# Expert rows fetched and results combined by indirect DMAs in place of one-hot products

## The chip, the cores and the metric

The kernel runs on one core of a Trainium2 chip, as one program. The metric is device microseconds. Engines are named as in the profile: PE is TensorE, PEld its weight loads, DVE is VectorE, ACT is ScalarE, POOL is GpSimd, and SP is SyncE, whose queue starts nearly all transfers.

## The reference

Two layers over 256 tokens of 1024 channels, all float32. Each layer mixes tokens and then channels; the first layer's channel part is dense, the second's is a mixture of eight experts of which each token takes two. Cut to what matters here:

```python
def swiglu(h, wg, wu, wd):
    return (jax.nn.silu(h @ wg) * (h @ wu)) @ wd

def moe(h, router, wg, wu, wd):
    logits = (h @ router).astype(jnp.float32)
    vals, idx = lax.top_k(logits, TOP_K)
    w = jax.nn.softmax(vals, axis=-1)
    gates = jnp.sum(jax.nn.one_hot(idx, N_EXPERTS, dtype=jnp.float32) * w[..., None], axis=-2)
    y = jnp.zeros_like(h)
    for e in range(N_EXPERTS):
        y = y + gates[..., e:e + 1].astype(h.dtype) * swiglu(h, wg[e], wu[e], wd[e])
    return y
...
        h = rmsnorm(x, ln2_g[l]) * (1.0 + sc2) + sh2
...
            f = moe(h, moe_router[j], moe_w_gate[j], moe_w_up[j], moe_w_down[j])
        x = x + g2 * f
    return rmsnorm(x, final_g)
```

An expert's three matrices are 1024 x 3072 each, 37.7 MB; all eight are 302 MB of the 424.68 MB that the page counts.

## The kernel before

**Weights.** All matrices stream from DRAM in chunks of 1 MB (128 x 2048 f32), in a fixed order, on SyncE's queue; `fetch` starts the next chunk, and the transfer waits there until the readers of its buffer are done. There are ten buffers named `raw`, one `raw2`, and one made of two halves (`raw3`, and the tile `xn1`): twelve in the experts. Where a product has three passes, each half chunk (512 KB, a *part*) is cut into a rounded `wh` by ScalarE (line 147) and a remainder `wl = raw - wh` by VectorE (line 148), the second part of the split. `split_next` issues the first; the second goes on the list `rests` and is issued by `split_rest`. `refill` keeps four parts cut ahead of TensorE, and issues the remainders of the earlier call, not its own; `piece` issues one if TensorE's program is about to need it. `mm3` (lines 208 to 210) makes wh, wl and the low part of the input into three passes.

**Order of the work.** No scheduler sets it. A tick (`tick`) is counted before each group of products; `after(n, fn)` puts work n ticks later, and `spread(ticks, steps)` runs the steps of a generator at such distances. What is issued at a tick stands in each engine's program there, and each engine runs its own program in order.

**Experts.** `route` computes the router, the two best experts of a token and their gates, and `sort` ranks the experts by their number of tokens, so that the slots j = 0 to 7 (E0 to E7 in this text) take them by size: slots 0, 2 and 3 are big (128 rows, three passes through wh and wl), 5 and 6 are middle ones (96 rows) and 1, 4 and 7 are half ones (64 rows). Middle and half experts multiply the f32 chunks as they lie (lines 889, 911, 942, 954, 974 and 981) and have no split. A big one has 72 ticks of six products, a half one 72 ticks, a middle one 84.

**Gather.** `gather` makes for one or two experts a one-hot of their rows (`pl`), multiplies the normed tokens, cut into `xh` and `xl`, by it (line 1484: 32 products of up to 256 columns), scales and shifts the result on ScalarE into the expert's inputs, and transposes the one-hots (lines 1500 and 1505) for the way back. It is called for E0 ahead of the loop, and in E0, E2, E4 and E6 for the two experts behind each (in E6 for E7 alone).

**Scatter.** When an expert's down products are done, `scatter` (line 1576, a big one), `scatter_half` (line 1525) or `scatter_mid` (line 1551) multiplies its result `y` by the transposed one-hot, and VectorE adds the product, times the token's gate, to the residual `x`. This is spread over the ticks of the next expert. E7's scatter, the norm and the output stand at the end. An overflow path, for more tokens than slots, stands behind and is not run with these inputs.

Of the kernel before, what the change touches and what calls it, by code (L numbers as in the profile page):

```python
# [49 lines left out]
QUAD = P // 4  # L50

# [17 lines left out]
C_ID, C_TRI, C_IOTA, C_SEL, C_TIE, C_PLACE = 0, 128, 256, 384, 388, 396  # L69
C_N = 404  # L70
# [4 lines left out]
class Kernel:  # L75
# [34 lines left out]
    def fetch(self):  # L110
# [3 lines left out]
        more = i % (RAW_BUFS + 2) - RAW_BUFS if i >= 0 else -1  # L114
# [3 lines left out]
        else:  # L118
            e[1] = [self.moe.tile([P, PIECE], F32, tag="raw3", name="raw", bufs=1),
                    self.core.tile([P, PIECE], F32, tag="xn1", name="raw")]  # L120
# [92 lines left out]
    def setup(self):  # L213
# [41 lines left out]
        self.places = cst[:, C_PLACE:C_PLACE + NE]  # L255
        self.par = par
# [1043 lines left out]
    def route(self, out):  # L1300
        nc, small = self.nc, self.small
        xh = [self.core.tile([P, D], F32R, tag=f"hh{t}", name="xh") for t in range(NT)]
        xl = [self.core.tile([P, D], F32R, tag=f"hl{t}", name="xl") for t in range(NT)]
# [21 lines left out]
        nc.scalar.activation(xh[0], out[0], AF.Copy)  # L1325
        gate2(4 - TICKS[1]["fill"][2])
        out.append(self.normed(1, y))
        modulated(0, ())
# [11 lines left out]
        nc.scalar.activation(xh[1], out[1], AF.Copy)  # L1340
# [3 lines left out]
        nc.vector.tensor_tensor(xl[0], out[0], xh[0].bitcast(F32), op=ALU.subtract)  # L1344
# [22 lines left out]
        nc.vector.tensor_tensor(xl[1], out[1], xh[1].bitcast(F32), op=ALU.subtract)  # L1367
# [13 lines left out]
        self.spread([9, 3], self.sort(mem))  # L1381
        return rank, gate, xh, xl
# [42 lines left out]

    def place(self, rank, e, base, out, dt_cols):
# [12 lines left out]
    def slots(self, single):  # L1439

        pl = self.work.tile([P, NT, 2 * P], F32R, tag="pl", name="pl", bufs=1)
        if single:
            self.nc.gpsimd.memset(pl[:, :, P:].bitcast(F32), 0.0)
        return pl

# [479 lines left out]
```

## Time and profile before

| | us |
|---|---|
| median of three runs | 1279.29 |
| lowest and highest | 1275.89, 1280.31 |
| the profiled execution | 1276.7 |
| its span | 1274.8 |
| TensorE busy | 1223.6 (96%) |
| VectorE busy | 687.7 (54%) |
| ScalarE busy | 554.2 (43%) |
| GpSimd busy | 21.3 (2%) |

The span is the profiled execution on the core; 1.9 us lie around it. Transfers moved 424.68 MB, 333 GB/s on average. Shares are averages over stages with different limits, so they are read by stretch.

The stages by time: layer 0's mix to 170 us, its dense part to 360, layer 1's mix to 486, the router to 507, then E0 to 617, E1 to 691, E2 to 797, E3 to 903, E4 to 977, E5 to 1081, E6 to 1185, and E7 with the end to 1274.8.

### The profile page before, as it was taken

Reading aid. Unit: us, or ns where it says so; the run is one execution under the profiler, and the core shown is the slowest. Engines: PE = TensorE matmul, PEld = TensorE weight load, DVE = VectorE, ACT = ScalarE, POOL = GpSimd, SP = SyncE. Lnnn points to the kernel's source line nnn. Section 1 sums busy time; section 2 is a strip of 40 time slices with the busy share of each in tenths; the row PEclk is TensorE's granted clock in tenths of the full one; section 3 lists DMA queues with packets and bytes.
Section 4 is the critical chain, followed back from the end, with each engine's and each line's share of the span. In section 5 each row is a group of like instructions: output and inputs, shape, how many; then the busy total and the mean of one; then the engine's idle time right before and its main releaser. Section 6 shows DMA issues by size and latency. Waiting matters only on the chain.

```text
span 1274.8 us, 19410 instructions
## 1 busy us (share of the span) xinstructions
PE 1223.6 (96%) x7702; PEld 813.0 (64%) x7702; DVE 687.7 (54%) x992; ACT 554.2 (43%) x809; POOL 21.3 (2%) x40
## 2 busy tenths in 40 slices
PE   5899999999999989999998999999999999999995
PEld 4777799999978768788434888888433333333332
DVE  4677687776567766988404889999401001100102
ACT  3466454444444945888203888788210000010001
POOL 1000100000000000000000000000000000000001
PEclk9999999999999988999999999999999999999998
DMA  9976788887544346899999999999999999998994
GB/s 374 418 304 229 275 315 300 308 298 293 191 183 168 131 171 256 300 338 343 364 418 419 419 418 419 391 363 366 343 419 418 418 419 417 364 375 348 418 418 194
DMA packets 63427, 424.68 MB, mean 333 GB/s; under 512 B 7734, under 2 KB 7990, under 8 KB 15072
## 3 DMA queue, kind: packets, MB, share of 16 engines
q1 hardware_dynamic: 63072, 423.28, 84.5%
q8 instruction: 62, 1.02, 0.3%
q14 instruction: 37, 0.30, 0.1%
q0 software_dynamic: 256, 0.09, 0.0%
HBM read 422.29 MB, written 1.05 MB: 332 GB/s over the span
## 4 chain that ended last, share of the span: by engine, by line
PE 81%; DMA 7%; DVE 6%; ACT 4%; issue 1%; SPq 0%; POOL 0%; POOLq 0%; DVEq 0%; ACTq 0%
PE gps L889 4%; PE ups L889 4%; PE gps L580 4%; PE gps L582 4%; PE gps L578 4%; PE gps L942 3%; PE yps L981 3%; PE ups L942 3%; PE bps L954 3%; DMA raw<-i_md 3%; DMA raw<-i_mu 3%; PE ups L209 2%; PE yps L209 2%; PE ups L208 2%; PE yps L210 2%; PE ups L210 2%
## 5 line engine op out<-in xcount | busy, mean ns | idle before, releaser
L148 DVE TENSOR_TENSOR wl<-raw,wh 128x1024 fp32r<-128x1024 f32 x344 | 408.2, 1220 | 57.6 <-ACT wh L147 55.3
L147 ACT ACTIVATE wh<-raw 128x1024 fp32r<-128x1024 f32 x344 | 359.7, 1060 | 168.0 <-PE gps L580 55.9
L580 PE MATMUL gps<-hl,wh 128*128 128x256 f32 x384 | 96.5, 284 | 0.7 <-DVE hl L566 0.7
L578 PE MATMUL gps<-hh,wh 128*128 128x256 f32 x384 | 96.7, 284 | 0.1
L580 PEld LDWEIGHTS gps<-hl,wh 128*128 128x128 f32 x384 | 72.8, 190 | 1.3 <-DVE hl L566 1.1
L578 PEld LDWEIGHTS gps<-hh,wh 128*128 128x128 f32 x384 | 72.8, 190 | 0.5 <-DVE hh L565 0.3
L900 DVE TENSOR_TENSOR sgs<-sgs,ups 128x512 f32<-128x512 f32 x9 | 6.2, 688 | 120.6 <-PE ups L889 120.6
L911 PE MATMUL yps<-raw,hTs 128*64 128x512 f32 x288 | 66.9, 596 | 2.3 <-DMA raw<-i_md 2.1
L947 DVE TENSOR_TENSOR sgm<-sgm,ups 128x512 f32<-128x512 f32 x6 | 4.1, 688 | 116.6 <-PE ups L942 116.6
L889 PE MATMUL ups<-raw,ef 128*64 128x512 f32 x288 | 65.3, 594 | 0.8 <-DMA raw<-i_mu 0.8
L889 PE MATMUL gps<-raw,ef 128*64 128x512 f32 x288 | 66.0, 598 | 0.0
L582 PE MATMUL gps<-hh,wl 128*128 128x256 f32 x384 | 61.7, 283 | 0.0
L209 PE MATMUL gps<-wl,eh 128*128 128x512 f32 x144 | 57.0, 396 | 1.5 <-DVE wl L148 1.5
L208 PE MATMUL gps<-wh,eh 128*128 128x512 f32 x144 | 57.0, 396 | 1.2 <-ACT wh L147 1.2
L208 PE MATMUL yps<-wh,fh 128*128 128x512 f32 x144 | 58.0, 402 | 0.0
L209 PE MATMUL ups<-wl,eh 128*128 128x512 f32 x144 | 56.9, 395 | 0.5 <-DVE wl L148 0.5
L209 PE MATMUL yps<-wl,fh 128*128 128x512 f32 x144 | 56.7, 394 | 0.4 <-DVE wl L148 0.3
L208 PE MATMUL ups<-wh,eh 128*128 128x512 f32 x144 | 56.9, 395 | 0.0
L210 PE MATMUL gps<-wh,el 128*128 128x512 f32 x144 | 56.4, 391 | 0.0
L210 PE MATMUL yps<-wh,fl 128*128 128x512 f32 x144 | 56.3, 391 | 0.0
L210 PE MATMUL ups<-wh,el 128*128 128x512 f32 x144 | 56.3, 391 | 0.0
L582 PEld LDWEIGHTS gps<-hh,wl 128*128 128x128 f32 x384 | 52.8, 190 | 0.0
(329 smaller groups left out, 2038.8 us busy)
## 6 DMA issues: line engine op xcount, KB each, us to landing
raw<-i_mu SPq DMA_DIRECT2D x92, 1024.0 KB, 10.5
raw<-i_md SPq DMA_DIRECT2D x88, 1024.0 KB, 11.8
raw<-i_mg SPq DMA_DIRECT2D x84, 1024.0 KB, 9.5
raw<-i_ada SPq DMA_DIRECT2D x48, 1024.0 KB, 7.5
raw<-i_win SPq DMA_DIRECT2D x20, 1024.0 KB, 9.2
raw<-i_fg SPq DMA_DIRECT2D x12, 1024.0 KB, 6.8
raw<-i_fu SPq DMA_DIRECT2D x12, 1024.0 KB, 6.9
raw<-i_fd SPq DMA_DIRECT2D x12, 1024.0 KB, 6.5
```

The lines of the kernel that those rows point to most:

```text
L147: nc.scalar.activation(wh, raw, AF.Copy)
L148: self.rests.append(lambda: nc.vector.tensor_tensor(wl, raw, wh.bitcast(F32), op=ALU.subtract))
L208: mm(out, lhsT=xh, rhs=wh, start=start, stop=False)
L209: mm(out, lhsT=xh, rhs=wl, start=False, stop=False)
L210: mm(out, lhsT=xl, rhs=wh, start=False, stop=stop)
L578: self.nc.tensor.matmul(out, lhsT=w, rhs=hh[:, k, :], stop=False, start=k == 0 and (len(ks) == NK or m + j == 0))
L580: self.nc.tensor.matmul(out, lhsT=w, rhs=hl[:, k, :], start=False, stop=False)
L582: self.nc.tensor.matmul(out, lhsT=wl[:, j * len(ks) + i, :], rhs=hh[:, k, :], start=False, stop=k == NK - 1 and (len(ks) == NK or m + j == 1))
L889: nc.tensor.matmul(ps[c * HALF:(c + 1) * HALF, :], lhsT=eh[:, k, :], rhs=w[c][i // 2][:, i % 2, :], start=k == 0, stop=k == NK - 1)
L911: self.nc.tensor.matmul(y[n * HALF:(n + 1) * HALF, :], lhsT=hT[:, b, c * HALF:(c + 1) * HALF], rhs=w[n][b // 2][:, b % 2, :], start=i == 0 ...
L942: nc.tensor.matmul(ps[q(2 * c + s), :], lhsT=eh[:, k, q(s)], rhs=ws[w][c][i // 2][:, i % 2, :], start=k == 0, stop=k == NK - 1)
L954: nc.tensor.matmul(bp[q(2 * w + c), :], lhsT=eh[:, k, q(2)], rhs=ws[w][c][i // 2][:, i % 2, :], start=k == 0, stop=k == NK - 1)
```

## The change

*Way in.* The normed tokens are written to DRAM (`rows_in`) as soon as they are there. `sort` makes, after the ranks, a list of token numbers for each slot (14 products of one column, `tokps`) and casts it to integers. The first expert is still gathered by one-hot products, in f32 and without the cut. For the others, GpSimd issues an indirect DMA that brings the slot's rows (64, 96 or 128 of 4 KB) from `rows_in` into `gx`; eight transposes on TensorE (line 1534) turn them, 12 ticks behind the issue for the first of a pair.

*Way out.* An expert's result is multiplied by the output gate and written to its place in `rows_out` in DRAM by GpSimd's DMAs. `sort` also computes for each token the two rows at which its results lie (`where`) and their gates (`mine`). In E7, six ticks in, four indirect DMAs of 128 rows bring these back; 28 ticks later VectorE adds them to `x` in four operations. E7's own result is still scattered by products.

*Weights.* A thirteenth buffer is made of the tiles `hl0` and `hl1`, which `xl` held. The remainder `wl` is issued by VectorE directly after its `wh`, not a `refill` later.

```diff
-GATHER = [18, 7, 10]
-SCATTER = [1, 1, 1, 3, 2, 2, 1, 1, 3, 2, 2]
-SCATTER_S = [1, 1, 1, 2, 2, 2, 2]
-SCATTER_M = [1, 2, 1, 2, 2, 2, 2]
+LISTS = [9, 3, 3, 2, 3]
+GATHER = [22, 12, 2, 3, 2, 3, 2]
+STORE = [1, 1, 2, 2]
+COMBINE = [6, 28, 1]
...
+SLOTS = [P if b else HALF + QUAD * m for b, m in zip(BIG, MID)]
+BASE = [sum(SLOTS[:j]) for j in range(NE)]
...
-        more = i % (RAW_BUFS + 2) - RAW_BUFS if i >= 0 else -1
+        more = i % (RAW_BUFS + 3) - RAW_BUFS if i >= 0 else -1
...
+            if more == 1:
+                e[1] = [self.core.tile([P, PIECE], F32, tag=f"hl{h}", name="raw") for h in range(2)]
...
     def piece(self, n):
-        if len(self.rests) >= len(self.ready):
-            self.split_rest()
         return [w.rearrange("p (a b) -> p a b", a=n) for w in self.ready.pop(0)]
     def refill(self, most=1 + AHEAD):
-
-        old = len(self.rests)
         while len(self.ready) < most and self.spos < self.limit and self.split_at(self.spos * PIECE // RAW):
-            self.split_next(False)
-        for _ in range(old):
-            self.split_rest()
+            self.split_next()
...
+        self.keep(0, out[0])
...
+        self.spread(LISTS, self.sort(mem))
...
+    def keep(self, t, xn):
...
+        self.nc.gpsimd.dma_start(self.rows_in[t * P:(t + 1) * P], xn)
...
+        one = [self.core.tile([P, NE, P], F32, tag=f"hh{t}", name="one") for t in range(NT)]
+        rankm = self.small.tile([P, NT, NE], F32, tag="rankm", name="rankm", bufs=1)
+        nc.vector.tensor_scalar(rankm, self.rankp, -1.0, None, op0=ALU.add)
+        for t in range(NT):
+            nc.vector.tensor_tensor(one[t], self.iota[:, None, :].to_broadcast([P, NE, P]),
+                                    rankm[:, t, :, None].to_broadcast([P, NE, P]), op=ALU.is_equal)
+        yield
+        ps = self.psum.tile([P, NE], F32, tag="tr", name="tokps")
+        for j in range(1, NE):
+            for t in range(NT):
+                nc.tensor.matmul(ps[:, j:j + 1], lhsT=one[t][:, j, :], rhs=self.tok[:, t:t + 1], start=t == 0, stop=t == 1)
+        self.tokens = const.tile([P, NE], U32, tag="tokens", name="tokens")
+        nc.vector.tensor_copy(self.tokens[:, 1:], ps[:, 1:])
...
+        for i in range(2):
+            eq = self.small.tile([P, NT, NE], F32, tag="eq", name="eq", bufs=1)
+            nc.vector.tensor_tensor(eq, key, top[:, :, i:i + 1].to_broadcast([P, NT, NE]), op=ALU.is_equal)
+            nc.vector.tensor_tensor(eq, eq, ok, op=ALU.mult)
+            nc.vector.tensor_reduce(self.mine[:, i, :], eq, axis=AX.X, op=ALU.add)
+            nc.vector.tensor_scalar(top[:, :, i:i + 1], top[:, :, i:i + 1], -1.0, 0.0, op0=ALU.add, op1=ALU.max)
+            nc.vector.tensor_copy(self.where[:, i, :], top[:, :, i])
...
-                for n, (src, t) in enumerate(((xh, 0), (xl, 0), (xh, 1), (xl, 1))):
-                    nc.tensor.matmul(ps[:, i, :], lhsT=src[t][:, bs], rhs=pl[:, t, :], start=(n == 0),
-                                     stop=(n == 3))
...
+                for t in range(NT):
+                    nc.tensor.matmul(ps[:, i, :], lhsT=xn[t][:, bs], rhs=pl[:, t, :], start=t == 0, stop=t == 1)
...
+    def gather(self, js):
+        nc, work = self.nc, self.work
+        got = []
         for n, j in enumerate(js):
-            if MID[j]:
-
-                tp = self.psum.tile([P, 2 * NT, P], F32, tag="tr", name="plT")
-                for t in range(NT):
-                    for i, w in enumerate((HALF, QUAD)):
-                        src = pl[:, t, n * P + i * HALF:n * P + i * HALF + w].bitcast(F32)
-                        for r in range(0, P, w):
-                            nc.tensor.matmul(tp[r:r + w, i * NT + t, :], lhsT=src, rhs=self.ident, start=True, stop=True)
-                pt = work.tile([P, 2 * NT, P], F32, tag="el", name="pt4", bufs=2)
-            else:
+            w = SLOTS[j]
+            gx = self.core.tile([P, D], F32, tag=f"hh{n}", name="gx")
+            nc.gpsimd.indirect_dma_start(gx[0:w], None, self.rows_in,
+                                         bass.IndirectOffsetOnAxis(ap=self.tokens[0:w, j:j + 1], axis=0))
+            got.append((gx, self.slot_tiles(j)))
+        yield
+        for (gx, outs), j in zip(got, js):
+            w = SLOTS[j]
+            pt = None
+            if j == NE - 1:
...
+            for h in range(0, NK, 4):
+                ps = self.psum.tile([P, 4, w], F32, tag="sc", name="gaps")
+                for i in range(4):
+                    nc.tensor.transpose(ps[:, i, :], gx[0:w, (h + i) * P:(h + i + 1) * P], self.ident[0:w, 0:w])
+                yield
+                for b in (0, 2):
+                    self.bring(j, outs, h + b, ps[:, b:b + 2, :])
+            self.taken[j] = outs, pt
...
+    def store_big(self, j, y):
+        nc = self.nc
+        o = self.core.tile([P, D], F32, tag="xn0", name="yo")
+        for n in range(2):
+            ns = slice(n * 512, (n + 1) * 512)
+            nc.vector.tensor_tensor(o[:, ns], y[n], self.g2[:, ns], op=ALU.mult)
+            if n == 0:
+                yield
+        nc.gpsimd.dma_start(self.rows_out[BASE[j]:BASE[j] + P], o)
...
+    def store_part(self, j, y, o, c):
+        nc = self.nc
+        for n in range(2):
+            rows = slice(n * HALF, (n + 1) * HALF)
+            ns = slice(n * 512, (n + 1) * 512)
+            nc.vector.tensor_tensor(o[rows, c:c + 512], y[rows], self.g2[rows, ns], op=ALU.mult)
+            nc.gpsimd.dma_start(self.rows_out[BASE[j]:BASE[j] + HALF, ns], o[rows, c:c + 512])
...
+    def combine(self):
+        nc = self.nc
+        got = []
+        for t in range(NT):
+            for i in range(2):
+                pool, tag, bufs = (self.work, "el", 2) if t else (self.core, f"hh{i}", None)
+                w = pool.tile([P, D], F32, tag=tag, name="yrow", **({"bufs": bufs} if bufs else {}))
+                nc.gpsimd.indirect_dma_start(w, None, self.rows_out,
+                                             bass.IndirectOffsetOnAxis(ap=self.where[:, i, t:t + 1], axis=0))
+                got.append(w)
+        yield
+        for t in range(NT):
+            for i in range(2):
+                nc.vector.scalar_tensor_tensor(self.x[:, t, :], got[2 * t + i], self.mine[:, i, t:t + 1], self.x[:, t, :],
+                                               op0=ALU.mult, op1=ALU.add)
+                yield
...
-                self.spread(GATHER, self.gather([i for i in (j + 1, j + 2) if i < NE], xh, xl))
+                self.spread(GATHER, self.gather([i for i in (j + 1, j + 2) if i < NE]))
...
+                self.spread(COMBINE, self.combine())
...
-                steps = self.scatter(j, y, pt, self.gatep)
+                steps = self.store_big(j, y)
...
-                steps = self.scatter_mid(j, y, pt)
+                steps = self.store_mid(j, y)
...
-                steps = self.scatter_half(j, y, pt, last)
+                steps = self.scatter_last(j, y, pt) if last else self.store_half(j, y)
```

**VectorE at the start.** Rows 47 to 57 of VectorE's program, in layer 0's first products; `set` and `nlam` are small arithmetic for the attention's lambda. Before:

```order
L286 TENSOR_SCALAR mask<-set_89 128x256 x2
L292 TENSOR_TENSOR set_90<-set_90 128x256
L294 TENSOR_REDUCE set_90<-set_90 128x4
L301 TENSOR_TENSOR nlam<-set_90 128x2
L303 TENSOR_SCALAR nlam<-nlam 128x1 x2
L305 TENSOR_SCALAR set_90<-set_90 128x8
L306 RECIPROCAL set_90<-set_90 128x8
L307 TENSOR_TENSOR set_90<-set_90 128x8
L308 TENSOR_TENSOR set_90<-set_90 128x8
L309 MEMSET set_90 128x8
L148 TENSOR_TENSOR wl<-raw,wh 128x1024 x2
```

The same rows now:

```order
L288 TENSOR_SCALAR mask<-set_89 128x256 x2
L153 TENSOR_TENSOR wl<-raw,wh 128x1024 x2
L294 TENSOR_TENSOR set_90<-set_90 128x256
L296 TENSOR_REDUCE set_90<-set_90 128x4
L303 TENSOR_TENSOR nlam<-set_90 128x2
L305 TENSOR_SCALAR nlam<-nlam 128x1 x2
L307 TENSOR_SCALAR set_90<-set_90 128x8
L308 RECIPROCAL set_90<-set_90 128x8
L309 TENSOR_TENSOR set_90<-set_90 128x8
L310 TENSOR_TENSOR set_90<-set_90 128x8
L311 MEMSET set_90 128x8
```

The two remainders stand ahead of the lambda arithmetic instead of behind it.

**VectorE in the first expert.** The end of `sort`, in E0: `most` is its last value before, `pl` the one-hots, `sg` and `fl` belong to the expert's own products. Before:

```order
L1423 TENSOR_SCALAR sort_5027<-sort_5027 128x1
L1424 CAST most<-sort_5027 128x1
L858 TENSOR_TENSOR sg<-sg,ups 128x512
L148 TENSOR_TENSOR wl<-raw,wh 128x1024
L1436 TENSOR_SCALAR pl<-cst,rankp 128x128 x2
L1429 TENSOR_SCALAR pl<-cst,rankp 128x128 x2
L148 TENSOR_TENSOR wl<-raw,wh 128x1024 x2
L566 TENSOR_TENSOR fl<-hT,fh 128x512
L148 TENSOR_TENSOR wl<-raw,wh 128x1024 x6
L566 TENSOR_TENSOR el<-ef,eh 128x256
```

The same place now, where `one` and `tokens` make the lists and `key` begins the 16 operations that compute `where` and `mine`:

```order
L1426 CAST most<-sort_5004 128x1
L1430 TENSOR_SCALAR rankm<-rankp 128x16
L1432 TENSOR_TENSOR one<-cst,rankm 128x1024 x2
L153 TENSOR_TENSOR wl<-raw,wh 128x1024
L860 TENSOR_TENSOR sg<-sg,ups 128x512
L153 TENSOR_TENSOR wl<-raw,wh 128x1024 x2
L1440 CAST tokens<-tokps 128x7
L153 TENSOR_TENSOR wl<-raw,wh 128x1024
L568 TENSOR_TENSOR fl<-hT,fh 128x512
L153 TENSOR_TENSOR wl<-raw,wh 128x1024 x2
L1445 TENSOR_TENSOR key<-rankp,cst 128x16
```

The four one-hot operations are gone; two wide compares and some 18 small operations stand between the remainders.

**TensorE in E4 and E5.** Line 911 is E4's down products, 942 E5's first ones, with transposes of one-hots and E4's scatter between. Before:

```order
L911 MATMUL yps<-raw,hTs 64x512 x12
L1500 MATMUL plT<-cst,pl 64x128 x2
L1500 MATMUL plT<-cst,pl 32x128 x4
L1500 MATMUL plT<-cst,pl 64x128 x2
L1500 MATMUL plT<-cst,pl 32x128 x4
L911 MATMUL yps<-raw,hTs 64x512 x16
L942 MATMUL gps<-raw,ef 32x512 x4
L1525 MATMUL scps<-yf,pt 128x512 x2
L942 MATMUL gps<-raw,ef 32x512 x4
L1500 MATMUL plT<-cst,pl 64x128 x2
L1500 MATMUL plT<-cst,pl 32x128 x4
L1500 MATMUL plT<-cst,pl 64x128 x2
```

The gather inside E4 now (lines 891, 899 and 913 are its products; 1534 turns the fetched rows of E5):

```order
L913 MATMUL yps<-raw,hTs 64x512 x2
L1534 MATMUL gaps<-cst,gx 128x96 x4
L913 MATMUL yps<-raw,hTs 64x512 x2
L899 MATMUL hTp<-cst,sgs 128x128 x4
L913 MATMUL yps<-raw,hTs 64x512 x2
L1534 MATMUL gaps<-cst,gx 128x96 x4
L913 MATMUL yps<-raw,hTs 64x512 x10
L1534 MATMUL gaps<-cst,gx 128x96 x4
L891 MATMUL gps<-raw,ef 64x512 x6
L1534 MATMUL gaps<-cst,gx 128x96 x4
L891 MATMUL gps<-raw,ef 64x512 x10
L891 MATMUL ups<-raw,ef 64x512 x16
```

The transposes of one-hots and the scatter products are gone from here; 16 transposes of fetched rows stand in E4 in place of its 32 one-hot products.

## Rows read from the trace of the kernel before

**Rows 1.** The page, the span in 40 equal slices of 31.9 us: busy tenths of TensorE and the GB/s that the core's transfers moved.

```profile
PE   5899999999999989999998999999999999999995
...
GB/s 374 418 304 229 275 315 300 308 298 293 191 183 168 131 171 256 300 338 343 364 418 419 419 418 419 391 363 366 343 419 418 418 419 417 364 375 348 418 418 194
```

**Rows 2.** The table by stretch, one stretch for an expert (the first, third, fifth and sixth of eight). Columns: stretch, its length, then the busy time of TensorE, of its weight loads, of VectorE, ScalarE and GpSimd (instructions in brackets), granted TensorE clock, DMA share, GB/s.

```profile
507.00:617.00 110.00, 108.69 (x501) 88.44 (x500) 97.75 (x125) 87.64 (x110) 0.00 (x0) 1.00 0.90 333
...
691.00:797.00 106.00, 106.00 (x486) 85.34 (x487) 95.56 (x100) 84.46 (x100) 0.00 (x0) 1.00 1.01 419
...
903.00:977.00 74.00, 74.00 (x367) 26.88 (x365) 7.05 (x13) 10.06 (x24) 0.00 (x0) 1.00 0.98 394
977.00:1081.00 104.00, 104.00 (x946) 31.57 (x945) 10.65 (x16) 7.10 (x13) 0.31 (x1) 1.00 1.01 418
```

**Rows 3.** The same table, cut where the rate of the transfers changes.

```profile
617.00:630.00 13.00, 13.00 (x59) 4.17 (x59) 2.79 (x4) 1.50 (x3) 0.00 (x0) 1.00 0.83 309
630.00:810.00 180.00, 176.36 (x803) 115.35 (x800) 114.30 (x120) 100.45 (x119) 0.00 (x0) 1.00 1.01 419
810.00:930.00 120.00, 120.00 (x541) 85.76 (x541) 91.79 (x93) 73.97 (x80) 0.00 (x0) 1.00 0.96 363
930.00:1080.00 150.00, 150.00 (x1182) 48.95 (x1182) 11.09 (x16) 14.83 (x33) 0.31 (x1) 1.00 1.01 418
1080.00:1170.00 90.00, 90.00 (x794) 29.74 (x790) 8.72 (x14) 9.46 (x21) 0.00 (x0) 1.00 0.90 358
```

**Rows 4.** The table of TensorE's waits from 680 to 692 us. Columns: who waits, for what, us in total, times, longest.

```profile
PE yps L911 <- DMA raw<-i_md: 1.3, 1, 1.3
PE gps L208 <- ACT wh L147: 1.2, 1, 1.2
PE gps L209 <- DVE wl L148: 1.0, 1, 1.0
```

**Rows 5.** The chain of work that ended last, from 1236 us to the end: start, duration, what.

```profile
1236.67 18.72 DMA raw<-i_md
...
1255.43 3.66 PE yps L911 x14
```

**Rows 6.** The same chain from 907 to 1083 us: scatter (scps), gather (gaps) transposes of one-hots (plT), and four transposes of f32 (hTp).

```profile
907.91 0.66 PE scps L1576 x2
...
928.20 1.15 PE gaps L1484 x8
...
938.08 1.11 PE gaps L1484 x8
...
962.95 0.59 PE hTp L897 x4
...
968.84 1.30 PE plT L1500 x24
...
979.05 1.06 PE scps L1525 x4
...
981.11 1.45 PE plT L1500 x24
...
1081.07 1.92 PE scps L1551 x8
```

**Rows 7.** The same chain from 485 to 520 us: the router's 32 products with eight columns, and a pair of transposes of one-hots.

```profile
492.77 5.18 PE lps L1323 x32
...
506.69 0.22 PE plT L1505 x2
```

**Rows 8.** DMA issues of the page: out<-in, queue, count, KB each, median us from issue to landing.

```profile
raw<-i_wout SPq DMA_DIRECT2D x8, 1024.0 KB, 5.3
...
row<-i_adab POOLq DMA_DIRECT2D x6, 8.0 KB, 5.2
```

**Rows 9.** The timeline from 28 to 59 us (in square brackets: idle time before, and what ended it).

```profile
28.99 2.36 DVE L148 TENSOR_TENSOR wl<-raw,wh 128x1024 fp32r<-128x1024 f32 x2
...
30.27 2.07 PE L596 MATMUL zps<-wl,hh 128*128 128x512 f32 x4 [2.99 <-DVE wl L148]
...
42.77 1.36 PE L596 MATMUL zps<-wl,hh 128*128 128x512 f32 x4 [2.50 <-DVE wl L148]
...
54.96 1.19 PE L596 MATMUL zps<-wl,hh 128*128 128x512 f32 x4 [2.04 <-DVE wl L148]
...
58.47 0.69 DVE L642 TENSOR_TENSOR rt<-zps,sincos 128x512 f32<-128x512 f32 x1 [0.15 <-PE zps L596]
```

**Rows 10.** The table of TensorE's waits from 60 to 120 us (first row) and from 405 to 455 us.

```profile
PE wops L209 <- DVE wl L148: 2.4, 1, 2.4
...
PE wops L209 <- DVE wl L148: 2.7, 1, 2.7
PE vps L209 <- DVE wl L148: 2.5, 1, 2.5
PE wops L208 <- DVE hh L565: 1.3, 1, 1.3
```

**Rows 11.** The table by stretch, in the first expert (columns as in rows 2).

```profile
525.00:540.00 15.00, 14.60 (x67) 11.44 (x67) 14.69 (x29) 11.63 (x13) 0.00 (x0) 1.00 0.81 296
```

**Rows 12.** DMA issues of the page between 1180 and 1260 us.

```profile
raw<-i_md SPq DMA_DIRECT2D x11, 1024.0 KB, 17.4
...
frow<-i_final_g POOLq DMA_DIRECT2D x1, 4.0 KB, 5.0
```

More of the change, by code (lines that the diff above doesn't have):

```diff
@@ new lines, in sort @@
+        yield
[6 more added lines that the diff above has]
+        yield
+        key, ok = [self.small.tile([P, NT, NE], F32, tag=f"key{i}", name="key", bufs=1) for i in range(2)]
@@ new lines, in sort @@
+        ts = lambda w: w[:, None, :].to_broadcast([P, NT, NE])
+        nc.vector.tensor_tensor(ok, self.rankp, ts(self.slots), op=ALU.is_le)
+        nc.vector.scalar_tensor_tensor(ok, self.rankp, 0.5, ok, op0=ALU.is_gt, op1=ALU.mult)
+        nc.vector.tensor_tensor(key, self.rankp, ts(self.base), op=ALU.add)
+        nc.vector.tensor_tensor(key, key, ok, op=ALU.mult)
+        top = self.small.tile([P, NT, 8], F32, tag="keys", name="keys", bufs=1)
+        for t in range(NT):
+            nc.vector.max(top[:, t, :], key[:, t, :])
@@ L1479, in gather, with gather_first @@
+    def gather_first(self, xn):
+        nc, work = self.nc, self.work
+        pl = work.tile([P, NT, P], F32, tag="pl", name="pl", bufs=1)
+        self.place(self.rank, 0, 0, pl, slice(0, P))
+        yield
+        outs = self.slot_tiles(0)
         for b in range(0, NK, 2):
[L1480 removed]
+            ps = self.psum.tile([P, 2, P], F32, tag="h", name="gaps")
             for i in range(2):
                 bs = slice((b + i) * P, (b + i + 1) * P)
[L1483 to L1485 removed]
@@ new lines, in store_part, with store_mid @@
+    def store_part(self, j, y, o, c):
+        nc = self.nc
+        for n in range(2):
[3 more added lines that the diff above has]
+            nc.gpsimd.dma_start(self.rows_out[BASE[j]:BASE[j] + HALF, ns], o[rows, c:c + 512])
+    def store_mid(self, j, y):
+        nc = self.nc
+        o = self.core.tile([P, D], F32, tag="xn0", name="yo")
+        odd = self.core.tile([P, 512], F32, tag="row2", name="yodd")
+        q = lambda i: slice(i * QUAD, (i + 1) * QUAD)
+        for n in range(2):
+            nc.scalar.activation(odd[q(2 * n)], y[1][q(2 * n + 1)], AF.Copy)
+        self.store_part(j, y[0], o, 0)
+        yield
+        for n in range(2):
+            ns = slice(n * 512, (n + 1) * 512)
+            rows = q(2 * n)
+            nc.vector.tensor_tensor(odd[rows], y[1][rows], odd[rows], op=ALU.add)
+            nc.vector.tensor_tensor(o[rows, 512:], odd[rows], self.g2[rows, ns], op=ALU.mult)
+            nc.gpsimd.dma_start(self.rows_out[BASE[j] + HALF:BASE[j] + HALF + QUAD, ns], o[rows, 512:])
+            yield
@@ L1523, in scatter_half @@
                 rows = slice(n * HALF, (n + 1) * HALF)
-                ps = self.psum.tile([P, 512], F32, tag="sc4" if last else "sc", name="scps")
-                nc.tensor.matmul(ps, lhsT=pt[rows, t, :].bitcast(F32), rhs=yf[rows], start=True, stop=True)
+                ps = self.psum.tile([P, 512], F32, tag="sc4", name="scps")
+                nc.tensor.matmul(ps, lhsT=pt[rows, t, :], rhs=yf[rows], start=True, stop=True)
                 pss[n] = ps
@@ L1531, in scatter_half @@
                                                op0=ALU.mult, op1=ALU.add)
[L1532 to L1556 removed]
+                self.sumsq(t, n)
             yield
@@ L1686, in stream_plain @@
                 bs = slice((b + i) * P, (b + i + 1) * P)
-                for n, (src, t) in enumerate(((xh, 0), (xl, 0), (xh, 1), (xl, 1))):
-                    nc.tensor.matmul(ps[:, i, :], lhsT=src[t][:, bs], rhs=pl[:, t, :], start=(n == 0),
-                                     stop=(n == 3))
+                for t in range(NT):
+                    nc.tensor.matmul(ps[:, i, :], lhsT=xn[t][:, bs], rhs=pl[:, t, :], start=t == 0, stop=t == 1)
             for i in range(4):
```

160 lines of the change are left out of this document (63 added, 97 removed).

## The prediction

> **What bounds the kernel now.** I read the slices of the page first [rows 1]: TensorE is busy in nearly every slice, and in the last twenty slices (from 637 us) the moved bytes sit at 418 or 419 GB/s in most, with two dips between. So in the experts (507 us to the end) two limits take turns, and the table by expert says which [rows 2]: the first expert (E0, 507 to 617) is TensorE's, with transfers at 333 GB/s; in the third (691 to 797) transfers run at 419 and TensorE is busy for all 106 us; in the fifth (903 to 977) 394 GB/s and again a full TensorE. Transfers and TensorE are almost level, with the weight buffers between them. Cut finer [rows 3], the transfers fall from 419 only in 617 to 630 (309 GB/s), 810 to 930 (363) and 1080 to 1170 (358). Elsewhere they run flat out while TensorE works off what the buffers hold. The waits of TensorE confirm it: at 680 to 692 it waits once for a weight chunk and twice for split parts [rows 4], then has no listed wait for 500 us. The chain at the end [rows 5] is a transfer of down weights that lands at 1255.4 and then 19.4 us of last matmuls, scatter and norm up to 1274.8. So the end is the transfers' end plus a tail; TensorE's work matters where a full set of buffers makes the transfers stop.
>
> All sums go against the profiled execution, 1276.7 us with a span of 1274.8; the median of the runs is 2.6 higher.
>
> **TensorE's work that goes.** From the chain [rows 6]: a one-hot gather of two experts is four groups at 1.11 to 1.15 us, three of them after 617 (13.6 us); transposes of the one-hots are 1.30 and 1.45 for the middle experts, and two of 128 columns took 0.22 [rows 7] for each of three others (0.7); scatters are four times 0.66 for each of three big experts (7.9), four times 1.06 for two half experts (4.2), four times 1.92 for two middle ones (7.7; the chain shows one such group). Together 36.8. Back come 40 transposes of 128 columns at most; four of those took 0.59 [rows 6], so 5.9. TensorE loses 31 us after 617, 28 of them after 691. VectorE and ScalarE lose scatter sums and copies there, but they are idle two thirds of the time or more in the experts without splits [rows 2], and I price that at nothing.
>
> **What a lighter TensorE gives the transfers.** The gaps of [rows 3] are (419-363)/419 x 120 = 16.0 us and (419-358)/419 x 90 = 13.1 us of transfer time lost to full buffers. (The 617 to 630 gap, 3.4 us, comes from before the removed work and stays.) Stretch by stretch: E2 and E3 need 212-8 = 204 us of TensorE against 180 us of weights and 4 of new bytes; the 20 us of surplus is about what the buffers took in before (16) plus 4, so the transfers hardly stop. E4 needs 68 against 93 and waits some 5 us at its end. E5 and E6 need 197 against 182, which fits the 12 buffers. So both gaps close: -29.1 us.
>
> **Bytes that are added.** Rows of 4 KB: the two copies of the rows out (1.05 MB) and the gathers for E1 and E2 (0.79) fall in E0, where the transfers have slack (333 GB/s). After it: gathers 0.79 + 0.79 + 0.26, stores of 704 rows 2.88, the combine's four times 128 rows 2.10: 6.82 MB. At 419 GB/s that is 16.3 us. No row shows an indirect transfer or one of this size beside the weights, so from both sides: 0 us if they go into gaps that I count as closed, 34 us at the rate of a lone 1 MB chunk (5.3 us, 198 GB/s [rows 8]). I take 16.3, since [rows 1] and [rows 3] never show over 419. The Trainium skill ("DMA: Bandwidth & Descriptors", section "Issuing engines are not separate DMA queues") says that DMAs started by different engines run on the same 16 DMA engines and interleave; by that rule 16.3 stands, without it 0 would be as likely. The rule speaks against the change, and [rows 3] agree in so far as no stretch goes above 419.
>
> **Thirteenth buffer, and split parts at once.** One chunk is 1.05 MB, 2.5 us at 419. The transfers can run one chunk further ahead, and the second split part at once frees a chunk half a chunk earlier (1.25 us): -3.75 where the lead is what ends last, 0 if the lead is never used up.
>
> In the layers before the experts, TensorE waits at the start three times for a second part that stands behind small operations on VectorE: 2.99, 2.50 and 2.04 us [rows 9]. In the new order the first moves ahead of the angle arithmetic, which begins 4 us sooner, and the second ahead of the lambda arithmetic, 2.4 us sooner; the third keeps its place behind small operations and stays. -5. What is put behind them is late by the 2.4 us of two parts; the angles are first read at 58.5 us. Later there is one wait of 2.4 and there are two of 2.7 and 2.5 for second parts [rows 10]; these may be taken over by the chain through VectorE that now has the part in front of TensorE's inputs, as in the 1.3 for a cut input in the same view. Ends +2 (every moved part delays an input once) and -10 (all go); I take -6 in all.
>
> **E0.** The first gather has 16 f32 products of 128 columns for 32 of 256 one-pass columns: even. Behind it the second and third experts' one-hot gather (four groups of 1.15, -4.6) and transposes (-0.4) go. New are 14 one-column f32 products for the lists; the router's 16 f32 products with eight columns stand as 32 records of 5.18 in all [rows 7], 0.32 a product, and one column can't cost more nor much less than a pair of transposes (0.22): 0.27 each, +3.8. New are 16 transposes at 0.59 per four, +2.4. New on VectorE are two 128x1024 compares (1.2 each as a second part, [rows 9]) and some 18 small operations at 0.16 to 0.24 between 525 and 540, where VectorE is busy 14.69 of 15 us [rows 11] and feeds the split parts: 5 to 6 us late against TensorE's lead of a few parts, +1 taken of a range 0 to +6. Sum +2.2, say +2.3; ends -3 and +6.
>
> **Sum.** Transfers' end 1255.4 - 29.1 + 16.3 - 3.75 - 6 + 2.3 = 1235.1; the tail of 19.4 is the same code (the combine stands in front of it, in E7, whose VectorE is free [rows 2]); span 1254.5, time 1256.4, and **1257** beside the median.
>
> **Rivals.** *TensorE stays the bound, the bytes are free.* If the new bytes go between the weights at no cost, the sum is without 16.3: 1240. For it: the transfer gaps; against: 419 is a ceiling everywhere.
>
> *The bytes cost double.* 34 us in place of 16.3: 1274.6, no gain to speak of. For it: rows of 4 KB in many small packets and the writes turn the direction; against: nothing in the rows but the 5.3 us of a lone chunk.
>
> *Gathered rows land late.* This ends slower. TensorE takes its instructions in order; the transposes stand 12 ticks behind the issue on GpSimd. By the ticks in an expert and its length [rows 2] (72 in 106 us for a big one, 72 in 74 for a half one, 84 in 104 for a middle one) a window is 17.7 us in E0 and in E2, 12.3 in E4, 14.9 in E6, 62.6 together. If a gather takes L, four cost 4L - 62.6, less the 16 us by which TensorE would be ahead of the transfers (1256 against 1240): it decides from L = 20 us, and is slower than before from 25; at 30 it is 41 on top, 1297. For it: SyncE's chunks of down weights take 17.4 us from issue to landing when its queue is full [rows 12]. Against: GpSimd's 8 KB took 5.2 [rows 8], and its 4 KB load in the very stretch of the 17.4 landed after 5.0, so its transfers don't stand in line behind the weights. The Trainium skill ("SBUF — State Buffer", section "SBUF: two separate sides") warns that GpSimd writes the descriptors of its DMAs itself and is locked out while VectorE runs certain wide copies. By that the gathers in E0 and E2, where VectorE is busy 90% [rows 2], would be the late ones. No row here shows such a stall.
>
> *The change does not do what it says.* If the chunk is still released by the split parts and not by TensorE, the 29 us stay lost and only bytes are added: 1276.7 + 16.3 - 6 - 3.75 + 2.3 = 1285.5. Against it: in the gap 1080 to 1170 no split runs at all.
>
> **Numbers.** The forecast 0.68; free bytes 0.13; double bytes 0.09 (half of it within 0.3% of before, which is 3.8 us and about what this kernel's runs can tell from no change); late rows 0.07; gaps stay 0.03. The forecast's own range is 1246 to 1268 (unknown costs at half their ends); with the free bytes below and the doubled ones above, 8 in 10 lie within 1240 to 1273. Faster 0.87, same 0.04, slower 0.09.
>
> **What would show it.** Right: 630 to the last chunk at 415 to 419 GB/s without a dip, though with more bytes; TensorE with a wait of some microseconds on down weights at the end of E4 and again in E7; no wait of the transposes of L1534 on a gather; the last chunk near 1235; the first second part wait at 30 us gone. Wrong: slices over 419, or dips still at 810 and 1080 (then TensorE is the bound), or a transpose that waits on GpSimd's queue. The prediction fails outright if the tail grows, as with a combine whose rows come after the last down weights.

## The result and the profile after

The median of four runs is 1261.3 us (1259.45 to 1262.55); the kernel before, beside it, took 1278.34 (1275.89 to 1280.31). The ratio is 0.9866, its interval 0.9844 to 0.9889. The profiled execution took 1260.87 us with a span of 1259.0.

The chain of the changed kernel at its end, for [rows 5]:

```profile
1224.50 14.90 DMA raw<-i_md
...
1239.44 3.66 PE yps L913 x14
```

The last chunk lands at 1239.40 in place of 1255.4, and the tail behind it is 19.6 us long (19.4 before). All of the gain is ahead of that chunk. The page's slices, for [rows 1], and its queues:

```profile
PE   6899999999999899999998999999998999999885
...
GB/s 378 419 371 208 328 269 326 315 299 270 167 224 161 101 201 349 307 321 353 360 419 410 418 419 420 420 419 419 372 419 419 418 418 419 404 419 416 419 420 152
...
q1 hardware_dynamic: 65952, 423.29, 84.5%
q0 software_dynamic: 2816, 8.74, 1.9%
```

The two dips of before, four slices and three slices long, are a slice each now, and TensorE is no longer full in the last slices. GpSimd's queue moved 8.74 MB. The table by stretch says where the 16 us came from. First the kernel before (E0; from E1's first product to the last chunk):

```profile
506.70:617.40 110.70, 109.39 (x504) 88.77 (x502) 98.05 (x126) 87.75 (x110) 0.00 (x0) 1.00 0.90 332
617.40:1255.40 638.00, 632.69 (x3803) 312.27 (x3802) 236.33 (x257) 204.97 (x263) 1.42 (x3) 1.00 0.98 397
```

and the same two stretches after:

```profile
493.10:610.00 116.90, 113.05 (x515) 91.77 (x513) 102.15 (x142) 87.60 (x108) 2.70 (x2) 0.97 0.90 341
610.00:1239.40 629.40, 606.83 (x3621) 299.00 (x3620) 222.77 (x220) 204.41 (x261) 18.95 (x26) 1.00 1.01 411
```

E0 begins 13.6 us earlier (493.1 against 506.7), takes 6.2 us more, and the rest takes 8.6 us less: -13.6 + 6.2 - 8.6 = -16.0. E0's start differs by some microseconds between executions: 492.4 to 496.7 us in the profiles of the ten kernels that issue the remainders at once, 506.7 and 506.9 in the two that don't. From E1 on, TensorE was busy for all but 5 of 638 us; now it is idle for 22.6 of 629.4, and waits for weights. In its table of waits from 480 to 1260 us:

```profile
PE yps L913 <- DMA raw<-i_md: 9.2, 8, 1.4
PE ups L891 <- DMA raw<-i_mu: 5.3, 3, 2.7
PE gps L891 <- DMA raw<-i_mg: 2.7, 2, 1.4
PE gps L208 <- DVE wl L153: 2.3, 1, 2.3
PE ups L944 <- DMA raw<-i_mu: 2.0, 2, 1.8
PE tokps L1438 <- DVE one L1432: 1.8, 2, 1.1
...
PE hT L865 <- DVE tokens L1440: 0.8, 1, 0.8
```

The bound behind E0 has thus moved from TensorE to the transfers. SyncE's queue says the same from the other side: from E1 to the end it waited 98.0 us for `bps` to leave a buffer before and 45.5 now, and 38.2 us in 23 waits for earlier down chunks before against 57.4 in 35 now.

The place where E0 loses its 6 us shows in TensorE's timeline (start, length, in brackets the idle time before and what ended it):

```profile
520.59 0.39 PE L209 MATMUL yps<-wh,fl 128*128 128x512 f32 x1
522.10 0.35 PE L1438 MATMUL tokps<-cst,one 128*128 128x1 f32 x2 [1.12 <-DVE one L1432]
523.15 3.31 PE L1438 MATMUL tokps<-cst,one 128*128 128x1 f32 x26 [0.69 <-DVE one L1432]
527.22 1.12 PE L865 MATMUL hT<-cst,sg 128*128 128x128 f32 x4 [0.77 <-DVE tokens L1440]
...
529.42 0.63 PE L207 MATMUL yps<-wh,fh 128*128 128x512 f32 x1
...
532.99 0.40 PE L207 MATMUL gps<-wh,eh 128*128 128x512 f32 x1
```

From 520.8 to 528.0 no product of the expert runs. TensorE waits for the compares, makes the lists, waits for their cast (they lie in the bank that the next transposes need), and then the expert's products run at 0.43 us apart until 532.4. The table by stretch gives the granted clock there and just behind:

```profile
528.00:532.40 4.40, 4.40 (x12) 3.44 (x11) 1.37 (x3) 1.65 (x2) 2.15 (x2) 0.50 1.01 415
533.00:537.00 4.00, 4.00 (x19) 3.33 (x18) 2.79 (x13) 3.19 (x3) 0.00 (x0) 1.00 1.04 312
```

0.50 is the lower of the two levels, 1.2 GHz, behind 6.4 us of waits and narrow products; at full clock those products stand 0.23 us apart. Ten of them at 0.20 more is 2 us.

### The profile page after: what moved, and what is told of

It is laid out like the page before. It is cut to its first block, busy times and chain, and to the rows that moved or that the text cites. A ratio compares the mean times of both kernels' runs of the same rounds, so it can differ in the third digit from the quotient of the medians.

```text
span 1259.0 us, 19199 instructions
## 1 busy us (share of the span) xinstructions
PE 1196.3 (95%) x7528; PEld 798.5 (63%) x7528; DVE 676.6 (54%) x969; ACT 550.0 (44%) x802; POOL 42.4 (3%) x66
## 3 DMA queue, kind: packets, MB, share of 16 engines
q0 software_dynamic: 2816, 8.74, 1.9%
HBM read 427.01 MB, written 4.98 MB: 343 GB/s over the span
## 4 chain that ended last, share of the span: by engine, by line
PE 72%; DMA 16%; DVE 5%; ACT 4%; issue 2%; POOL 0%; SPq 0%; POOLq 0%; ACTq 0%; DVEq 0%
DMA raw<-i_md 8%; DMA raw<-i_mu 4%; PE gps L582 4%; PE gps L584 4%; PE gps L580 4%; PE yps L983 3%; PE ups L944 3%; PE bps L956 3%; PE gps L944 3%; PE yps L207 2%; PE yps L209 2%; PE yps L208 2%; PE ups L208 2%; PE ups L209 2%; PE ups L207 2%; PE gps L208 2%
## 5 line engine op out<-in xcount | busy, mean ns | idle before, releaser
L153 DVE TENSOR_TENSOR wl<-raw,wh 128x1024 fp32r<-128x1024 f32 x344 | 414.1, 1222 | 93.6 <-ACT wh L152 85.0
L913 PE MATMUL yps<-raw,hTs 128*64 128x512 f32 x288 | 72.6, 599 | 9.3 <-DMA raw<-i_md 9.2
L207 PE MATMUL gps<-wh,eh 128*128 128x512 f32 x144 | 57.4, 399 | 0.0
L913 PEld LDWEIGHTS yps<-raw,hTs 128*64 128x64 f32 x288 | 22.8, 136 | 51.7 <-issue 30.6
## 6 DMA issues: line engine op xcount, KB each, us to landing
raw<-i_mg SPq DMA_DIRECT2D x28, 512.0 KB, 16.3
```

Source lines behind the costliest of these rows:

```text
L153: self.rests.append(lambda: nc.vector.tensor_tensor(wl, raw, wh.bitcast(F32), op=ALU.subtract))
L207: mm(out, lhsT=xh, rhs=wh, start=start, stop=False)
L913: self.nc.tensor.matmul(y[n * HALF:(n + 1) * HALF, :], lhsT=hT[:, b, c * HALF:(c + 1) * HALF], rhs=w[n][b // 2][:, b % 2, :], start=i == 0 ...
```

## The experiments

All kernels are told as median and ratio to the kernel before beside them, with its interval. E0 is told by its first product and its length.

**The split alone (e1).** The kernel before, with only the remainders issued at once:

```diff
-            self.split_next(False)
-        for _ in range(old):
-            self.split_rest()
+            self.split_next()
```

> The kernel before with one part of the change: each remainder wl is issued by VectorE right behind its wh; gather, scatter and the twelve buffers stay. Theory (what is saved ahead of the experts is carried to the end): the changed kernel begins E0 at 493.1 us against 506.7 and its list of waits has lost the second parts, so this kernel should begin E0 13 us earlier too, at 493 to 495, and take 1264 to 1267 us. Rival 1 (half of the 13.6 us comes from the cuts xh and xl that the change leaves out of the router): E0 at 499 to 501, 1270 to 1273 us. Rival 2 (the experts are bound by the transfers, which catch up and give it back): E0 at 494, but over 1274 us.

1262.44 us (1260.85 to 1266.16), ratio 0.9899 (0.9868 to 0.993). E0 begins at 492.4. Both lie a little under the theory's ranges, by 1.6 and 0.6 us.

```profile
492.40:602.70 110.30, 108.89 (x507) 88.89 (x505) 97.61 (x125) 87.77 (x111) 0.00 (x0) 1.00 0.91 336
602.70:1239.60 636.90, 631.81 (x3803) 312.71 (x3802) 237.46 (x257) 204.53 (x263) 1.42 (x3) 1.00 0.98 397
```

The stretch from E1 on is as before: TensorE full, 397 GB/s. The 14.3 us ahead of E0 arrive at the end undiminished (the last chunk lands at 1239.6). And this is the time of the whole change, within the intervals. The theory holds but for these margins, and both rivals fall.

**All but the split (e2).** The changed kernel with the remainders deferred as before:

```diff
-            self.split_next()
+            self.split_next(False)
+        for _ in range(old):
+            self.split_rest()
```

> The changed kernel with the remainders deferred to the next refill as before. Theory: E0 begins at 504 to 507 us, and as the rest of the change is worth only some 4 us, the time is 1271 to 1275 us. Rival 1 (half of the gain ahead of the experts comes from the cuts xh and xl that are gone): E0 at 499 to 501, 1266 to 1269 us. Rival 2 (what is lost ahead of the experts comes back, as the transfers are what ends): under 1265 us.

1277.52 us (1274.36 to 1279.47, 10 runs), ratio 0.9996 (0.9981 to 1.001): nothing is left. The theory expected some 4 us from the rest of the change, and there were none.

```profile
506.90:627.90 121.00, 116.03 (x514) 94.56 (x513) 102.17 (x142) 87.64 (x108) 2.70 (x2) 0.94 0.87 322
627.90:1256.20 628.30, 606.72 (x3621) 299.26 (x3620) 220.76 (x220) 204.40 (x261) 18.88 (x26) 1.00 1.01 412
```

Its two halves are there all the same. E0 begins at 506.9, as before, and takes 121.0 us (+10.3); the rest, to the last chunk, takes 628.3 (-9.7). Fetching the rows, with the thirteenth buffer, gains some 10 us behind E0 and loses as much in it.

**Twelve buffers (e3).**

```diff
-        more = i % (RAW_BUFS + 3) - RAW_BUFS if i >= 0 else -1
+        more = i % (RAW_BUFS + 2) - RAW_BUFS if i >= 0 else -1
```

> The changed kernel with twelve weight buffers in place of thirteen (the tiles hl0 and hl1 stay unused). Theory (from the end of E0 the transfers are the bound and the lead that the buffers hold is what ends last): one chunk less, 2.5 to 3.5 us later, 1264 to 1265 us. Rival (TensorE is the bound and the lead is never used up): 1261 us, no change.

1262.86 us (1261.71 to 1264.55), ratio 0.989 (0.9861 to 0.9918). 1.6 us more than the changed kernel, less than expected, with intervals that overlap: the thirteenth buffer's gain isn't told apart from none. Its profiled execution, at 1264.55 the longest of the four, lost 3.6 us ahead of E0 (which begins at 496.7), where this edit changes nothing, and only half a microsecond from E1 to the end.

**No way out (e4).** Neither `self.spread(STORE, steps)` nor `self.spread(COMBINE, self.combine())`.

> The changed kernel without the way out: the results of E0 to E6 are neither stored nor fetched and added, so the output lacks those seven experts. Taken away are 2.88 MB of stores, 2.10 MB of fetches (4.98 MB), and the multiplications by the output gate. Theory (transfers are the bound, and bytes cost what they cost at 419 GB/s, or at 365 as the page's share of the software queue has it): 12 to 13.6 us less in transfers, 1248 to 1250 us, unless TensorE becomes the bound sooner. Rival (the bytes fit into gaps that are there anyway): 1259 to 1262 us.

1248.42 us (1245.54 to 1250.58), ratio 0.9776 (0.9744 to 0.9809): 12.9 us less for 4.98 MB, 2.6 us per MB, as the theory says. The stretch from E1 to the last chunk, where E0's start doesn't enter, is 14.2 us shorter than the 629.4 of the changed kernel, 2.9 per MB:

```profile
612.00:1227.20 615.20, 601.78 (x3621) 298.23 (x3620) 203.66 (x195) 201.71 (x257) 4.57 (x5) 1.00 1.01 412
```

**The combine's fetches twice (e6).**

```diff
...
-                nc.gpsimd.indirect_dma_start(w, None, self.rows_out,
-                                             bass.IndirectOffsetOnAxis(ap=self.where[:, i, t:t + 1], axis=0))
+                for _ in range(2):
+                    nc.gpsimd.indirect_dma_start(w, None, self.rows_out,
+                                                 bass.IndirectOffsetOnAxis(ap=self.where[:, i, t:t + 1], axis=0))
...
```

> The changed kernel with each of the four fetches of the combine issued twice into the same tile: 2.10 MB more in E7. Theory (bytes in the transfer-bound part cost what they cost without the way out, 12.9 us for 4.98 MB, or 2.6 us per MB): 5.0 to 5.5 us more, 1266 to 1267 us. Rival 1 (they find gaps): 1261 us. Rival 2 (the second fetches, in order on GpSimd behind the first, hold up the sums and the end): over 1270 us.

1267.17 us (1265.78 to 1267.83), ratio 0.9923 (0.9893 to 0.9953): 5.9 us for 2.10 MB, 2.8 per MB. From E1 to the last chunk it is 5.6 us longer, 2.7 per MB:

```profile
610.60:1245.60 635.00, 612.55 (x3621) 299.24 (x3620) 222.80 (x220) 204.37 (x261) 22.61 (x30) 0.99 1.01 411
```

Adding bytes and taking them away give nearly the same price. It isn't sharper than that: by the ratios to the kernel before beside each, e4 gives 2.3 and e6 3.5, give or take 1 and 2.3. The last chunk lands 6.2 us later than in the changed kernel, and the tail stays, so the sums don't hold up the end.

**Lists spread (e5).**

```diff
-LISTS = [9, 3, 3, 2, 3]
-GATHER = [22, 12, 2, 3, 2, 3, 2]
+LISTS = [9, 3, 3, 2, 7, 1, 1, 1, 1, 1, 1, 3]
+GATHER = [34, 12, 2, 3, 2, 3, 2]
...
-        ps = self.psum.tile([P, NE], F32, tag="tr", name="tokps")
+        ps = self.psum.tile([P, NE], F32, tag="h", name="tokps")
...
+            if j + 1 < NE:
+                yield
```

> The changed kernel with the 14 list products, which stand in a row in E0 three ticks behind the compares, set 7 ticks behind them and two to a tick, between the expert's own products, in a bank of their own; the fetches of E1 and E2 (and of later pairs) follow at tick 34 in place of 22. Theory (the lists are what takes back the gain in E0: TensorE waits for the compares, the narrow products run at about half the granted clock and the 4.8 us of products behind them too): E0 takes 110 to 112 us in place of 116.9, and all of it is carried to the end: 1255 to 1257 us. Rival 1 (E0 is longer by the 16 transposes and VectorE's small operations): E0 115 to 117, 1260 to 1262 us. Rival 2 (the transfers, the bound from E1 on, take back what E0 wins): E0 111, but 1259 to 1262 us.

1262.12 us (1260.18 to 1262.92), ratio 0.9882 (0.9852 to 0.9913): a miss, at the figures of rival 1 (which names the transposes and VectorE's small operations). The lists' products, two to a tick, ran at full clock and waited for nothing. Yet E0 took 117.0 us. TensorE's longest wait in E0 is now:

```profile
PE hT L865 <- DVE sg L860: 3.9, 1, 3.9
```

The transposes wait for the gate product `sg`, which stands behind the two wide compares (2.36 us) and the remainders on VectorE. TensorE has to wait there anyway; in the changed kernel the list products stand in that wait. (The expectation has the narrow products themselves at about half the clock. In the changed kernel 0.92 was granted among them; 0.50 came only behind them.)

**No list products (e7).** The 14 products left out, each list the numbers 0 to 127.

> The changed kernel without the 14 list products: the compares stay, and each list is the numbers 0 to 127, so that the wrong tokens are fetched for E1 to E7, as many rows and bytes as before. It gives the price of the products by themselves. Theory: E0 loses the 7.2 us from the last product before them to the first behind and 2.4 us of slower products behind: 107 to 108 us long, 1251 to 1253 us. Rival (VectorE's work in E0 sets its length): E0 over 112, over 1256 us.

1257.01 us (1256.28 to 1259.52), ratio 0.9843 (0.9814 to 0.9872). E0 took 113.5 us, not 107 to 108, and TensorE waited the same 3.9 us for `sg`:

```profile
494.30:607.80 113.50, 108.39 (x487) 87.40 (x485) 101.82 (x141) 87.54 (x108) 2.58 (x2) 0.98 0.92 347
```

These are the rival's figures: VectorE's work sets E0's length here. The products by themselves cost 3.4 us of E0 (4.3 of the time), and what is left over the 110.3 us of e1 is about this wait.

**Other lists in E1 (e8).** In E0 the lists of E1 and E2 alone; compares, products and the arithmetic of the way back for the others in E1, where VectorE has little to do:

```diff
...
+        for lo, hi, tag in ((1, 3, "h"), (3, NE, "sc")):
+            one = [self.core.tile([P, hi - lo, P], F32, tag=f"hh{t}", name="one") for t in range(NT)]
...
```

> The changed kernel with the lists of E1 and E2 alone in E0 (four products, compares of 256 columns), 6 ticks behind the compares; the compares and ten products of the other lists, and the arithmetic for the way back, stand in E1, one list to a tick; fetches at tick 32. Theory (TensorE is the bound up to the end of E0, the transfers behind it, so that TensorE's work costs in E0 and not in E1): E0 107.5 to 110 us, 1252 to 1255 us. Rival (work moved to E1 costs there what it cost in E0): the time of the kernel with the spread lists, or more.

1254.81 us (1254.16 to 1257.68), ratio 0.9835 (0.9803 to 0.9866).

```profile
604.00:1233.10 629.10, 611.81 (x3643) 301.64 (x3642) 226.54 (x240) 204.02 (x261) 18.89 (x26) 0.99 1.01 412
493.50:604.00 110.50, 107.44 (x495) 87.14 (x493) 99.55 (x126) 87.61 (x108) 1.98 (x2) 1.00 0.94 353
```

E0 is at 110.5, as in e1 and half a microsecond over what was expected, and the stretch behind it is as long as in the changed kernel, though 5 us of TensorE's work were moved into it. So work in E0 lengthened the kernel, and behind E0 there was room for it.

**The sort's other parts in E1 too (e9).** As e8, with the permuted gates and the overflow count behind the first lists:

```diff
-LISTS = [9, 3, 3, 2, 3]
+LISTS = [9, 3, 5, 6, 1, 56, 2, 4, 1, 1, 1, 1, 3]
...
+            if lo == 1:
+                permute(self.gate, self.gatep)
...
```

> The kernel with the other lists in E1, and in addition the permuted gates and the eight operations of the overflow count moved from E0 into E1 (12 small operations, some 2.2 us of VectorE at a place where the gate product sg comes late and TensorE's transposes wait 2.3 us for it). Theory (TensorE's wait for VectorE in E0 is the last of the change's cost there): E0 108 to 109 us in place of 110.5, 1252 to 1253.5 us. Rival (the wait is set by the remainders that now stand ahead of sg, not by the small operations): E0 stays at 110.5, 1254 to 1256 us.

1252.32 us (1251.9 to 1256.82, 5 runs), ratio 0.9812 (0.9789 to 0.9836): E0 108.3 us, and its wait for `sg` is 0.5 in place of e8's 2.3:

```profile
493.90:602.20 108.30, 107.09 (x495) 87.33 (x493) 97.00 (x112) 87.50 (x108) 1.98 (x2) 1.00 0.95 365
```

As expected, VectorE's small operations were what was left in E0. The times of e8 and e9 alone, whose intervals overlap, would not tell them apart. This is the fastest kernel here that computes everything; it beats both the kernel before and the changed one.

**The way out by products (e10).** As e8, with one-hots, their transposes and the scatters back for the way out, and no stores or combine; the other lists stand 20 ticks later than in e8.

> The kernel with the other lists in E1, with the way in by fetches and the way out as before by one-hot products (one-hots, their transposes and the scatters back; no stores, no combine): 4.98 MB less, and 20 us of scatter products and 4 us of transposes more on TensorE. Theory (from E1 on TensorE and the transfers are nearly level, so that neither way out is worth much against the other): TensorE's 631.8 us in the kernel with the split alone, less 13.6 of gathers, plus 5.9 of transposes and 2 of lists is 626, against 629 from E1 to the last chunk with both ways by fetches: 1250 to 1256 us. Rival 1 (the transfers are the bound and the bytes are won in full): 1242 to 1244 us. Rival 2 (the way out is what pays in the change): 1259 to 1263 us, as with the split alone.

1255.66 us (1254.32 to 1256.54), ratio 0.9831 (0.9808 to 0.9854), the time of e8.

```profile
493.20:604.30 111.10, 108.03 (x501) 87.71 (x499) 100.65 (x130) 88.64 (x112) 1.96 (x2) 1.00 0.95 354
604.30:1233.20 628.90, 624.63 (x3765) 305.46 (x3764) 239.38 (x256) 205.76 (x266) 5.93 (x7) 1.00 0.99 403
```

TensorE is busy for 624.6 us (626 expected) and the bytes are fewer (403 GB/s): the same length, with the other limit. Against e8 TensorE is 12.8 us busier, where the expectation's products come to 24; why isn't shown. The way out by fetches is worth nothing here. The way in seems to pay: this kernel is 6.8 us under e1, which has both ways by products, but the thirteenth buffer is in that difference too, and no run takes the two apart.

## Why the prediction was right, and where not

The time came out within 0.3% (1257 against 1261.3), by terms that were off in both directions, so the closeness is in good part luck. (By the 2.6 us that the prediction itself puts between the profiled execution and the median, its 1256.4 would read 1259 beside the median, not 1257.)

*Ahead of E0: forecast -6, measured -13.6.* The waits at the start came out as forecast: three of 7.5 us together are one of 2.0, -5.5 against -5. Of the 7.6 us of later waits the prediction let only 1 go; all went. In their place came waits of 2.7 for `pTs`, 1.0 for `row` and 0.5 for `mx`; the 1.3 for `hh` became 0.5 and 0.8. Now the table of TensorE's waits ahead of E0 begins, behind one of 9.5 that was 9.7:

```profile
PE pT L770 <- ACT pTs L773: 2.7, 1, 2.7
PE zps L598 <- DVE wl L153: 2.0, 1, 2.0
PE wops L207 <- DVE hh L567: 1.3, 2, 0.8
PE zps L595 <- DVE hl L568: 1.1, 1, 1.1
PE colps L417 <- DVE row L410: 1.0, 1, 1.0
```

Together TensorE is idle for 23.0 us ahead of E0 in place of 31.5.

That is 8.5 of the 13.6. The other 5.1 are busy time, which the prediction left at nothing. Products behind two of the first waits ran at a lower clock before. The records behind the first and the second wait, 69 each, before (columns as in the table by stretch):

```profile
30.30:34.70 4.40, 4.40 (x69) 3.28 (x69) 1.05 (x1) 0.00 (x0) 0.00 (x0) 0.64 1.02 411
42.80:47.40 4.60, 4.60 (x69) 3.56 (x69) 1.05 (x1) 0.00 (x0) 0.00 (x0) 0.63 1.03 426
```

and after, where these two waits are gone:

```profile
29.00:31.90 2.90, 2.90 (x69) 2.25 (x67) 2.56 (x14) 0.26 (x1) 0.00 (x0) 1.00 0.98 405
38.70:41.80 3.10, 3.05 (x69) 2.40 (x69) 2.69 (x9) 0.51 (x3) 0.00 (x0) 1.00 1.01 423
```

These two places are 3.0 of the 5.1 us; where the rest lies isn't followed here. e1 shows that the split alone does all this (TensorE busy for 469.5 us ahead of E0 against 475.2, with as many products), and with it nearly the whole result.

*E0: forecast +2.3, measured +6.2.* The term that was mis-sized is the +1 for VectorE. The +3.8 for the list products held: their 28 records took 3.7 us, and without them (e7) E0 is 3.4 shorter. But e7 is still 2.8 us longer than before, where the transposes less the one-hot work that went make it 2.6 shorter (2.4 - 5.0), so what hangs on VectorE cost 5.4: the compares and small operations held up `sg`, TensorE waited, and the products behind ran at half the clock. The range named for VectorE, 0 to 6, held it; the value was taken too near its lower end. With e9, where most of this is moved, E0 is 108.3 us long, 2.4 shorter than before.

*From E1 to the last chunk: forecast -16.55, measured -8.6.* The bytes came out as forecast: 411 GB/s x 629.4 us is 258.7 MB, 5.4 MB more than before, 12.9 us at 419; forecast were 16.3 - 3.75 = 12.55. The 3.75 is less sure: e3 shows 1.6 for the buffer (2.5 forecast), within its noise, and e1's stretch is 1.1 us shorter by the earlier release (1.25 forecast). The free-bytes rival is out (e4, e6), and so is the doubled price of 5.0 us per MB (e4). The term that was too large is the 29.1 for the gaps: at 419, 33.5 us of transfer time were lost before and 12.0 after, so 21.5 came back. Of the 12.0, 3.1 are the part that was expected to stay (400 GB/s from 610 to 679) and 3.5 a rest of the first gap at the start of E4 (399). 3.0 stand in E7 (403), nearly all in the last 4.4 us of the stream, at 143 GB/s. TensorE also lost less than forecast, 25.9 us of busy time in place of 31. By e10's measure most of what was to be won from E1 on is won: with 12.8 us of TensorE's work given back (624.6 against 611.8), the stretch has the same length.

*The rivals.* Gathered rows never were late: no wait of the transposes of L1534 is in the tables, and the page has for the fetches

```profile
gx<-rows_in,tokens POOLq DMA_INDIRECT x7, 7.8
...
yrow<-rows_out,where POOLq DMA_INDIRECT x4, 12.3
```

7.8 us (12.1 the longest) against windows of 12 us and more. The Trainium skill's warning ("SBUF — State Buffer", section "SBUF: two separate sides") on descriptors that GpSimd can't write while VectorE runs certain copies did not show as a late row. It was hardly put to the test: VectorE's work in E0 and E2 is mostly remainders, subtractions of two tiles, and not copies. The fetches held GpSimd for 1.72 and 0.98 us in E0, 1.00 and 1.90 in E2, 0.97 and 0.95 in E4, and no transpose waited for one. The Trainium skill's rule that DMAs of all engines run on the same 16 ("DMA: Bandwidth & Descriptors", section "Issuing engines are not separate DMA queues") agrees with e4 and e6, at 2.6 and 2.8 us per MB.

Of the signs that the prediction named, TensorE's waits at the end of E4 (3.9 us idle) and in E7 (11.0) came, and the first wait for a remainder is gone. The mean from 630 on at 415 to 419 GB/s without a dip did not quite come: a slice is at 372 and one at 404, and the mean from E1 on is 411. The last chunk landed at 1239.4, not 1235.1.

What the prediction had as its argument, that the time follows from fetched rows and closed gaps, is therefore not what made the time. Fetched rows with the thirteenth buffer (e2) are worth 0; the issue order of VectorE alone (e1) is worth 14.8 us of the 17. Errors of 7.6 us ahead of E0 and 8.0 behind it cancelled, and E0's 3.9 is what is left with them.

## What to carry to other kernels

When a change has several parts, price each against the bound of its own stretch: here a few waits of 2 to 3 us ahead of the experts, with the lower clock behind some of them, were worth more than 26 us of TensorE's work (632.7 us down to 606.8) in stretches where the transfers stand right behind it. Work for a later stage belongs where the engine that does it has room (here the lists in E1, not in E0), and spreading the products doesn't help while the operations that feed them stay in the way. Moving work from TensorE to bytes pays only until the other limit is reached; after that the way that needs less code is as good.

## What the runs showed of the hardware

The indirect fetches of 4 KB rows and the stores run beside a full stream of weights and cost little more than their bytes: 8.74 MB in 1.9% of the 16 engines' span, 23.9 us by the page, 365 GB/s. Products of one column, 26 records, took 3.31 us, 0.13 each, where they stood in a row after a wait, and the clock was granted at 0.50 for the 4.4 us behind. In e5 it was 0.50 for 2.8 us behind 3.9 us of plain waiting, with no narrow product near, so the wait alone was enough. At the start of the kernel before it was 0.64 and 0.63 in 4.4 and 4.6 us behind waits of 2.99 and 2.50; behind the third, 2.04 us, it stayed at 1.00. Each of these two waits cost 1.5 us more in the products behind it (4.4 and 4.6 us in place of 2.9 and 3.1).
